# The output stage of a hybrid decoder layer in another written order

## The chip, the core and the metric

The kernel runs on one core of a Trainium2 chip. A core has five engines with queues of their own, which meet only through semaphores: TensorE (PE, matrix products into PSUM), VectorE (DVE), ScalarE (ACT), GpSimd (POOL) and SyncE (SP, which issues most DMAs). Each engine takes its instructions strictly in the order in which the program holds them. The metric is the device time of one execution in microseconds, the median of several runs.

## What is computed

One layer of a decoder, on 1024 positions of width 1024. Cut to what matters here:

```python
m = sigmoid(g_att) * y_att + sigmoid(g_conv) * y_conv
x = x + rms_norm(m @ w_out, norm_mix_post)
h = rms_norm(x, norm_ffn_pre)
a, g = split(causal_dwconv(h @ w_up, conv_ffn_w), 2)
x = x + rms_norm((gelu(g) * a) @ w_down, norm_ffn_post)
```

The change concerns the second and third line, and how the first columns of the fourth are begun.

## The kernel before

All products run in float16, with each operand split in a high and a low half (`hi = f16(s*x)`, `lo = f16(s*x - hi)`) and three products high·high, high·low, low·high (`PASSES`) per pair of tiles. Weights are scaled by a power of two that comes from the sum of their squares. Splitting takes a ScalarE copy (L100) and a VectorE subtraction (L101).

The up-projection uses a two by two block scheme with seven products in place of eight. A `Pair` (class at the end of the file) holds one column tile of `a` and one of `g`; `mm(i)` issues product i (12 matmuls of 128x512, L1682), `take(i)` evicts it. The block operands are the first and second half of the positions (tokens 0 to 3 and 4 to 7, where a token means 128 positions) and of the columns, and sums and differences of these. They lie transposed in `hA` (plain blocks) and `hB` (three sums).

The output stage (end of `mixer`, from L1085) makes these operands. For each token it does

- the product with `w_out`: two halves of 512 columns, each 24 matmuls into one PSUM bank `py` (L1104);
- `taken`: for each half, ScalarE sums the squares (L1111) and VectorE multiplies by the gain into `hn` (L1113);
- `root`: a small VectorE add (L1121, second time L1118) and a power on GpSimd (L1122, L1119);
- `resid`: `x = hn * root + xr`, with `xr` loaded into a weight tile (pool `ws`) and the sum in a tile of pool `xp`, then its store for the last stage (L1126, L1127);
- `squared` (L1130), the second `root`, and `normed`, which gives the normalised row again in `hn` (L1134).

What follows depends on the token. Tokens 0 to 2 are "light": split and transposed by DMA into `hA`. Tokens 4 to 6 are "heavy" (`heavy`): four differences with the light partner, five splits into high (`high`) and low half (`low`), five DMA transposes. Tokens 3 and 7 are transposed on PE (`turned`, L1197) and their halves, sums and differences written from PSUM by ScalarE and VectorE, because they come last. At the same time the weights of the first two pairs, u0 and u1, are split; u1 is loaded, its squares are summed (L57), added up over the partitions by a matmul with ones (`pr`, L83), and split.

What sets the order: the whole stage stands in a `manual_schedule` for PE, ACT, DVE and SP, so the written order is the order on every engine. The tokens come as `seq = (0, 4, 1, 5, 2, 6, 3, 7)`. Operations are called in groups; the steps of `heavy` wait in a list `todo` and are taken from it by `drain(n)` at fixed places of the loop over the tokens. The pool `xp` has four tiles, two of which hold gains throughout the stage; `ws` has four, PSUM eight banks, of which a token takes two.

Of the kernel before, what the change touches and what calls it, by code (L numbers as in the profile page):

```python
# [16 lines left out]
F16 = mybir.dt.float16  # L17
# [17 lines left out]
ENGINES = {mybir.EngineType.PE, mybir.EngineType.Activation, mybir.EngineType.DVE, mybir.EngineType.SP}  # L35
PASSES = ((0, 0), (0, 1), (1, 0))


class Layer:
# [290 lines left out]
    def mixer(self, mid):  # L330
# [753 lines left out]
        seq = (0, 4, 1, 5, 2, 6, 3, 7)  # L1084
        xr, h, sq, ps, y = {}, {}, {}, {}, {}  # L1085
        todo = []

        def drain(n):
            for f in todo[:n]:
                f()  # L1090
            del todo[:n]
# [15 lines left out]
        def taken(tt, nh):  # L1107
# [3 lines left out]
            nc.scalar.activation(self.junk(f"jk_n_post{tt}_{nh}")[:, sl], ps[tt][nh], AF.Square, scale=sgn[:, 25:26],  # L1111
                                 accum_out=sq[tt][:, nh:nh + 1])
            nc.vector.scalar_tensor_tensor(h[tt][:, sl], ps[tt][nh], sgn[:, 24:25], gp_[:, sl], ALU.mult, ALU.mult)  # L1113
# [10 lines left out]
        def resid(tt):  # L1124
            y[tt] = self.xp.tile([P, D], F32, tag="x", name=f"x2_{tt}")
            nc.vector.scalar_tensor_tensor(y[tt], h[tt], sq[tt][:, 3:4], xr[tt], ALU.mult, ALU.add)  # L1126
            nc.sync.dma_start(self.x2[tt], y[tt])  # L1127
# [17 lines left out]
        def light_low(tt):  # L1145
            sub_(hs[tt][:, :, 1], h[tt].rearrange("p (a c) -> p a c", a=2), hs[tt][:, :, 0])
            nc.sync.dma_start_transpose(hA.rearrange("p a l k t -> p (a l k) t")[:, :, ds(tt * P, P)],
                                        hs[tt].rearrange("p a l c -> p (a l c)"))

        def heavy(tt):  # L1150

            A, B = h[tt], h[tt - 4]
# [12 lines left out]
            def high(n, src):  # L1165
                nc.scalar.activation(half(n)[:, :NH], src, AF.Copy)

            def low(n, src):
                sub_(half(n)[:, NH:], src, half(n)[:, :NH])
                nc.sync.dma_start_transpose(dst[n], half(n))  # L1170

            def first():
                sub_(B[:, lo_], A[:, lo_], B[:, lo_])
                high(0, B[:, lo_])

            def second():
                st["c"] = self.wh.tile([P, D], F32, tag="wh", name=f"hs{tt}c")
                sub_(st["c"][:, lo_], A[:, hi_], B[:, lo_])
                high(1, st["c"][:, lo_])
                high(4, A[:, hi_])  # L1180

            def third():
                sub_(A[:, lo_], A[:, hi_], A[:, lo_])
                high(2, A[:, lo_])

            def fourth():
                sub_(B[:, hi_], B[:, hi_], st["c"][:, lo_])
                high(3, B[:, hi_])
            todo.extend([first, second, lambda: low(0, B[:, lo_]), third, lambda: low(1, st["c"][:, lo_]), fourth,
                         lambda: low(4, A[:, hi_]), lambda: low(2, A[:, lo_]), lambda: low(3, B[:, hi_])])  # L1190

# [9 lines left out]

        with tc.manual_schedule(engines=ENGINES):
            load_xr(0)
            load_xr(4)
# [22 lines left out]
            load_xr(1)  # L1227
            begin(1)
            products(1, 0, range(8))
            for tt in (0, 4):  # L1230
                taken(tt, 0), taken(tt, 1)
                root(tt, False)
            resid(0), squared(0)
            resid(4), squared(4)
            root(0, True)
            taken(1, 0)
            normed(0)
            root(4, True)
            light_high(0)
            normed(4)  # L1240
            light_low(0)
            products(1, 1, range(8))
            heavy(4)
            drain(1)
            for m in range(3, 8):
                t, prev = seq[m], seq[m - 1]
                begin(t)
                if m == 6:
                    r = self.scale_sum(sm_u1, 2)
                products(t, 0, range(8))  # L1250
# [24 lines left out]
                root(prev, True)
                if m == 6:
                    self.pair_first("u1")
                drain(1)
                taken(t, 0)
                if m == 5:  # L1280
                    self.sumsq(raw[1], sm_u1[:, 1:2], "u1_1")
                normed(prev)
                if prev == 3:
                    drain(2)
                elif prev < 4:
                    light_high(prev)
                    drain(2)
                    light_low(prev)
                    drain(1)
                else:  # L1290
                    if m == 6:
                        self.pair_sums("u1", self.ws.tile([P, D], F32, tag="ws", name="s12_u1"))
                    heavy(prev)
                    drain(3)
            products(7, 1, range(5))
            turned(3)
            products(7, 1, range(5, 8))
            s3, s7 = ds(3 * P, P), ds(NH + 3 * P, P)

            def b_high(e):  # L1300
                nc.scalar.activation(hA[:, e, 0, :, s3], k_t(pt[3][e]), AF.Copy)

            def b_low(e):
                sub_(hA[:, e, 1, :, s3], k_t(pt[3][e]), hA[:, e, 0, :, s3])
            b_high(0)
            taken(7, 1)
            b_low(0)
            p0.mm(1)
            root(7, False)
            b_high(1)  # L1310
            hq = self.slot([P, 2, KH, P], F32, "hq")
            nc.scalar.activation(hq[:, 0], k_t(pt[3][0]), AF.Copy)
            b_low(1)
            drain(2)
            resid(7)
            p0.take(1)
            squared(7)
            self.pair_part("u1", 2)
            root(7, True)
            p1.mm(1)  # L1320
            p1.take(1)
            normed(7)
            p0.mm(2)
            p0.take(2)
            turned(7)
            p1.mm(2)
            q0, q1 = pt[7]
            tb = [self.slot([P, 2, KH, P], F32, f"tb{e}") for e in range(2)]
# [486 lines left out]
```

## Time and profile before

| | us |
|---|---|
| three runs | 1300.84, 1303.78, 1303.88 (median 1303.78) |
| the profiled execution | 1305.98 |
| its span | 1304.2 |
| mean granted TensorE clock in it | 0.994 |

The span goes from the first to the last instruction of the program in the profile; the time of the execution has 1.8 us around it. In the profile's lists, `x384` is a count, names left of `<-` are written and those right of it read, buffer numbers are left out, and L1104 is a line of the kernel. A bracket at the end of a timeline row holds the idle time of the engine ahead of that row and what ended it. In the table by stretches each engine has its busy time and, behind the x, its instructions; the last three columns are the granted TensorE clock as a share of full speed, the DMA engines' busy share and GB/s.

The page's section 4 follows the work back from the last instruction:

```profile
PE 86%; DVE 8%; ACT 3%; issue 2%; DMA 1%; POOL 0%; SPq 0%; POOLq 0%; DVEq 0%; ACTq 0%
```

The chain runs over TensorE for most of the span; the rest are the places where it waits for the others.

### The profile page before, as it was taken

What the parts mean: (1) busy time and instruction counts of PE and PEld (TensorE: products, weight loads), DVE (VectorE), ACT (ScalarE), POOL (GpSimd) and SP (SyncE); (2) the same over time, 40 slices, a digit from 0 to 9 for tenths busy, and PEclk for the clock granted to TensorE, in tenths of its full rate; (3) what the DMA queues carried; (4) which work ended last, traced back from release to release, by engine and by line L of the source; (5) the groups of instructions that cost most, each with busy time, mean ns of one, the idle gap of its engine ahead of it and who ended that gap; (6) DMA issues with size and microseconds to landing.
All of it is one profiled execution on the core that took longest, in us unless ns stands there. A gap on an engine that the chain in (4) does not pass through costs nothing.

```text
span 1304.2 us, 16771 instructions
## 1 busy us (share of the span) xinstructions
PE 1279.6 (98%) x6450; PEld 581.4 (45%) x6450; DVE 993.5 (76%) x1571; ACT 800.1 (61%) x1136; POOL 48.1 (4%) x67
## 2 busy tenths in 40 slices
PE   9999999999999999999879999999999999999997
PEld 4444444444444444444334444444444444444443
DVE  7488788888878788787768959917963891799767
ACT  6466666665777756654445767746763764677422
POOL 2000000000000000001100000010011001000001
PEclk9999999999999999999989999999999999999999
DMA  6345454453432122516732252274247228622125
GB/s 260 81 81 113 85 119 101 112 111 79 106 100 65 49 81 70 184 32 152 184 106 89 74 232 66 76 135 145 65 116 174 66 72 212 201 65 97 65 98 177
DMA packets 139888, 146.66 MB, mean 112 GB/s; under 512 B 109592, under 2 KB 109728, under 8 KB 139808
## 3 DMA queue, kind: packets, MB, share of 16 engines
q1 hardware_dynamic: 135904, 131.43, 34.6%
q0 software_dynamic: 3888, 14.16, 5.9%
q8 instruction: 50, 0.82, 0.2%
q14 instruction: 30, 0.25, 0.1%
q10 hardware_dynamic: 16, 0.00, 0.0%
HBM read 93.93 MB, written 25.17 MB: 91 GB/s over the span
## 4 chain that ended last, share of the span: by engine, by line
PE 86%; DVE 8%; ACT 3%; issue 2%; DMA 1%; POOL 0%; SPq 0%; POOLq 0%; DVEq 0%; ACTq 0%
PE pd L1488 14%; PE pq L262 3%; PE pcc L262 3%; PE pk L262 3%; PE pywa L662 3%; PE py L1104 3%; PE pywc L662 3%; PE pd L1529 3%; PE pcx L262 2%; PE pcb L262 2%; PE pv L397 2%; PE z L690 2%; PE o L753 2%; DVE R L708 1%; PE pw L420 1%
## 5 line engine op out<-in xcount | busy, mean ns | idle before, releaser
L1682 PEld LDWEIGHTS <-wh_u 128*128 128x128 f16 x1848 | 179.2, 98 | 217.8 <-issue 4.6
L1488 PE MATMUL pd<-wdh,f 128*128 128x512 f16 x864 | 188.8, 379 | 1.2 <-ACT wdh L100 1.2
L1488 PEld LDWEIGHTS <-f 128*128 128x128 f16 x864 | 84.4, 98 | 103.7 <-issue 2.3
L1682 PEld LDWEIGHTS <-wh_g 128*128 128x128 f16 x588 | 56.9, 98 | 68.6 <-issue 0.4
L1104 PE MATMUL py<-wh_wo,m 128*128 128x512 f16 x384 | 86.2, 387 | 0.4 <-DVE wh_wo L101 0.4
L101 DVE SCALAR_TENSOR_TENSOR wh_u<-ws_u,sc,wh_u 128x1024 f16<-128x1024 f32 (+1 forms) x66 | 72.3, 1099 | 11.4 <-ACT wh_u L100 11.4
L100 ACT ACTIVATE wh_u<-ws_u,sc 128x1024 f16<-128x1024 f32 (+1 forms) x66 | 64.5, 998 | 26.4 <-DVE sc L92 12.9
L1502 ACT ACTIVATE y<-pd,sd 128x512 f32<-128x512 f32 x64 | 42.1, 697 | 60.5 <-PE pd L1488 54.0
L694 ACT ACTIVATE R<-z,cz 128x1024 f32<-128x1024 f32 (+3 forms) x48 | 43.1, 898 | 46.5 <-PE z L690 46.5
L1762 DVE SCALAR_TENSOR_TENSOR ugu<-cgu,cw_g,ugu 128x1023 f32<-128x1023 f32 (+1 forms) x44 | 56.3, 1278 | 11.3 <-ACT ugu L1760 11.1
L708 DVE TENSOR_TENSOR_SCAN R<-R,edge 128x256 f32<-128x256 f32 (+3 forms) x64 | 49.2, 810 | 19.3 <-ACT R L694 19.1
L1104 PEld LDWEIGHTS <-m 128*128 128x128 f16 x384 | 38.2, 100 | 51.2 <-issue 8.0
L90 DVE TENSOR_SCALAR sc<-pr 128x1 int32<-128x1 int32 x45 | 6.4, 151 | 71.0 <-PE pr L83 71.0
L1762 DVE SCALAR_TENSOR_TENSOR ua<-cau,cw_a,ua 128x1023 f32<-128x1023 f32 (+1 forms) x44 | 56.2, 1277 | 2.0 <-ACT ua L1760 1.9
L57 ACT ACTIVATE jk_u<-ws_u 128x1024 bf16<-128x1024 f32 x44 | 46.5, 1058 | 4.9 <-DMA ws_u<-w_up_nt 4.3
L695 ACT ACTIVATE be<-z,cz 128x1024 f32<-128x1024 f32 (+3 forms) x48 | 43.0, 896 | 9.4 <-DVE R L727 9.3
L708 DVE TENSOR_TENSOR_SCAN R<-R,cy,zero 128x512 f32<-128x512 f32 x32 | 39.3, 1270 | 10.7 <-ACT R L694 10.7
L717 DVE TENSOR_TENSOR be<-be,R 128x1024 f32<-128x1024 f32 (+3 forms) x48 | 45.7, 951 | 0.1
L727 DVE TENSOR_TENSOR R<-be,R 128x1024 f16<-128x1024 f32 (+3 forms) x48 | 45.7, 951 | 0.0
L262 PE MATMUL pcx<-hT,wh_cx 128*128 128x512 f16 x192 | 44.2, 380 | 0.0
L262 PE MATMUL pcb<-hT,wh_cb 128*128 128x512 f16 x192 | 44.2, 380 | 0.0
L262 PE MATMUL pq<-hT,wh_q 128*128 128x512 f16 x192 | 44.1, 380 | 0.0
(718 smaller groups left out, 2552.3 us busy)
## 6 DMA issues: line engine op xcount, KB each, us to landing
ws_u<-w_up_nt SPq DMA_DIRECT2D x44, 512.0 KB, 3.5
yd<-y POOLq DMA_DIRECT2D x24, 512.0 KB, 5.5
ds<-w_down SPq DMA_DIRECT2D x22, 512.0 KB, 5.6
wd<-w_down SPq DMA_DIRECT2D x22, 512.0 KB, 3.6
ws_g<-w_in_nt SPq DMA_DIRECT2D x14, 512.0 KB, 3.5
x<-x SPq DMA_DIRECT2D x8, 512.0 KB, 10.0
ws_wo<-w_out SPq DMA_DIRECT2D x8, 512.0 KB, 6.1
xr<-x SPq DMA_DIRECT2D x8, 512.0 KB, 3.9
```

What stands on the lines that cost most here:

```text
L57: self.nc.scalar.activation(self.junk(f"jk_{name}")[:, :w], src, AF.Square, accum_out=acc)
L100: self.nc.scalar.activation(dst[:, 0, :], src, AF.Copy, scale=s)
L101: self.nc.vector.scalar_tensor_tensor(dst[:, 1, :], src, s, dst[:, 0, :], ALU.mult, ALU.subtract)
L262: nc.tensor.matmul(ps, w[:, wi, ds(k * P, P)], hT[:, hi, k, ds(c * NH, NH)], start=n == 0, stop=n == last)
L662: nc.tensor.matmul(ps, w[0][:, wi, ds((d % 2) * NH + k * P, P)], acts[bi][k][:, hi, ds(c * NH, NH)], start=n == 0, stop=n == 11)
L708: nc.vector.tensor_tensor_scan(rev, rev, first, 0.0 if u["top"] else carry[tl][:, h, :], ALU.mult, ALU.add)
L717: nc.vector.tensor_tensor(t["be"][:, :, :W], t["be"][:, :, :W], t["R"][:, :, 1:W + 1], ALU.mult)
L727: nc.vector.tensor_tensor(wv[1], be[:, :, :W], wv[0], ALU.subtract)
L1104: nc.tensor.matmul(ps[tt][nh], m16[k][:, hi, ds(tt * P, P)], wo[k][:, wi, ds(nh * NH, NH)], start=k == 0 and p == 0, stop=k == 7 and p == 2)
L1488: nc.tensor.matmul(banks[n][:, :cw], f16[g][k][:, hi, ds(tt * P, P)], w[k][:, wi, ds(c0, cw)], start=(hi, wi) == (0, 0) and k == 0, stop=( ...
L1682: nc.tensor.matmul(ps, w[wt][:, wi, ds(wc * NH + k * P, P)], l.block(i, hi, k), start=first and n == 0, stop=n == 3 * KH - 1, skip_group_c ...
L1762: nc.vector.scalar_tensor_tensor(u[:, lag:], c[:, :T - lag], sm[:, 2 - lag:3 - lag], u[:, lag:], ALU.mult, ALU.add)
```

## The change

The groups of the stage are taken apart into single operations, each with a short name in a table `op`: `P31` is the second half of token 3's product, `q` the sum of squares of a half, `g` its gain, `r`/`R` the two roots, `x` the residual, `Y` its store, `s` the second square, `n` the normed row, `X` the load; `H`, `L`, `D` a light token's high half, low half and transpose; `a` to `d`, `h`, `l`, `D` with a number a heavy token's; `T` the transposes on PE; `u`, `v` the weight parts of the first two pairs; `p` and `E` products and evictions of these pairs. A list of 225 names gives the order, and a loop runs through it. The tokens come as 0, 1, 4, 5, 3, 2, 6, 7. The residual's input is loaded into the tile that takes the sum; for the first two tokens that is a `ws` tile, for the others one of `xp`. Before the list stand only the last parts of `w_out` and the products of tokens 0 and 1, interleaved by k.

```diff
+TOKENS = (0, 1, 4, 5, 3, 2, 6, 7)
+OUT_ORDER = (
...
+    "d5 D51 h53 l53 D54 n3 P60 q21 r2 g21 D53 x2 Y2 s2 X6 P61 j0 R2 j1 n2 q60 ut H2 g60 v1 L2 T3 X7 q61 "
+    "v2 D2 um P70 th0 r6 g61 th1 tl0 up tq x6 vh0 tl1 Y6 s6 vl0 P71 q70 R6 v3 v4 g70 n6 a6 b6 h60 c6 h61 "
+    "p01 l60 q71 l61 D60 vh2 r7 g71 h62 vl2 p11 E01 h64 x7 vh3 l62 Y7 s7 p02 l64 D62 d6 E11 R7 vl3 D61 "
+    "h63 l63 E02 D64 n7 T7 p12 t1 D63 t2 k1 tr e1 k2 t3 p05 vh1 e2 t4 k3 k5 e3 k4 vl1 p15 E12 E05 e5 e4 "
+    "E15 "
+)
...
-        seq = (0, 4, 1, 5, 2, 6, 3, 7)
...
         def load_xr(tt):
-            xr[tt] = self.ws.tile([P, D], F32, tag="ws", name=f"xr{tt}")
-            nc.sync.dma_start(xr[tt], a["x"][ds(tt * P, P), :])
+            n = TOKENS.index(tt)
+            pool, tag = (self.ws, "ws") if n < 2 else (self.xp, "x")
+            y[tt] = pool.tile([P, D], F32, tag=tag, name=f"x2_{tt}")
+            nc.sync.dma_start(y[tt], a["x"][ds(tt * P, P), :])
...
         def resid(tt):
-            y[tt] = self.xp.tile([P, D], F32, tag="x", name=f"x2_{tt}")
-            nc.vector.scalar_tensor_tensor(y[tt], h[tt], sq[tt][:, 3:4], xr[tt], ALU.mult, ALU.add)
+            nc.vector.scalar_tensor_tensor(y[tt], h[tt], sq[tt][:, 3:4], y[tt], ALU.mult, ALU.add)
+
+        def stored(tt):
             nc.sync.dma_start(self.x2[tt], y[tt])
...
+        def part_high(n, i, pool, tag):
+            w = pool.tile([P, 2, D], F16, tag=tag, name=f"wh_{n}_{i}")
+            self.pw[n][0][i] = w[:, :, :NH] if i == 3 else w
+            nc.scalar.activation(self.pw[n][0][i][:, 0], source(n, i), AF.Copy, scale=self.pscale[n])
+
+        def part_low(n, i):
+            w = self.pw[n][0][i]
+            nc.vector.scalar_tensor_tensor(w[:, 1], source(n, i), self.pscale[n], w[:, 0], ALU.mult, ALU.subtract)
...
-            self.pair_first("u0")
-            for i in (2, 1, 3):
-                self.pair_part("u0", i)
-            begin(0), begin(4)
+            for tt in TOKENS:
+                begin(tt)
             for k in range(8):
-                for tt in (0, 4):
+                for tt in TOKENS[:2]:
                     for nh in range(2):
                         products(tt, nh, [k])
...
-            for m in range(3, 8):
-                t, prev = seq[m], seq[m - 1]
...
-            products(7, 1, range(5))
-            turned(3)
-            products(7, 1, range(5, 8))
...
+            for name in OUT_ORDER.split():
+                op[name]()
             self.pair_fetch("u2")
```

Every engine holds the same instructions as before, and up to the stage and behind it in the same order. Three places show what moves. The names below are the program's: `py_0`, `py_1` the two halves of a token's product, `pt` the transposes on PE, `pr` the sum for u1's scale, `m_k` the k-th tile of the left operand.

TensorE before, at the sum for the scale, which stands between the two halves of token 3 (`py_0_5832`, `py_1_5833`), and then at token 3's transposes, which stand inside the second half of token 7 (`py_1_5928`):

```order
L1104 MATMUL py_0_5832<-wh_wo_5347,m_7_5338 128x512
L83 LDWEIGHTS ones
L83 MATMUL pr_5862<-rb_5835,ones 128x1
L1104 LDWEIGHTS m_0_4508
L1104 MATMUL py_1_5833<-wh_wo_5258,m_0_4508 128x512
```

```order
L1104 MATMUL py_1_5928<-wh_wo_5334,m_4_4875 128x512
L1197 MATMUL pt_0_6000<-ident,hn_5908 128x128 x4
L1197 MATMUL pt_1_6001<-ident,hn_5908 128x128 x4
L1104 LDWEIGHTS m_5_5060
L1104 MATMUL py_1_5928<-wh_wo_5340,m_5_5060 128x512
```

TensorE now, behind the second half of token 6 (`py_1_5370`) and ahead of token 7 (`py_0_5372`), where token 3 is `hn_5760`:

```order
L1111 MATMUL py_1_5370<-wh_wo_5347,m_7_5338 128x512
L1210 MATMUL pt_0_5903<-ident,hn_5760 128x128 x4
L1210 MATMUL pt_1_5904<-ident,hn_5760 128x128 x4
L95 LDWEIGHTS ones
L95 MATMUL pr_5919<-rb_5893,ones 128x1
L1111 LDWEIGHTS m_0_4508
L1111 MATMUL py_0_5372<-wh_wo_5258,m_0_4508 128x512
```

Both have one place now, 14 halves into the stage: the sum comes one half later than before, the transposes one half and 15 matmuls earlier, while token 3's own products come four halves earlier.

VectorE before, from the gain of token 7's second half (`hn_5976`) to its normed row and the first reader of its transposes (`tb`):

```order
L1113 SCALAR_TENSOR_TENSOR hn_5976<-py_1_5928,sgn,g_post 128x512
L1137 TENSOR_TENSOR hA<-pt_0_6000,hA 128x4x128
L1121 TENSOR_SCALAR r_post_5926<-r_post_5926 128x1
L1137 TENSOR_TENSOR hA<-pt_1_6001,hA 128x4x128
L1126 SCALAR_TENSOR_TENSOR x_7_6043<-hn_5976,r_post_5926,xr_5966 128x1024
L101 SCALAR_TENSOR_TENSOR wh_u_2_6051<-s_u_5913,sc_5834,wh_u_2_6051 128x1024
L1118 TENSOR_SCALAR r_post_5926<-r_post_5926 128x1
L1134 SCALAR_TENSOR_TENSOR hn_5976<-x_7_6043,r_post_5926,g_ffn 128x1024
L1137 TENSOR_TENSOR tb_6108<-pt_0_6086,hq 128x512
```

VectorE now, at the same place (token 7 is `hn_5994`; `hs6b`, `hs6c` and `hn_5806` are halves of token 6's operands):

```order
L1131 TENSOR_SCALAR r_post_5371<-r_post_5371 128x1
L1123 SCALAR_TENSOR_TENSOR hn_5994<-py_1_5373,sgn,g_post 128x512
L1275 SCALAR_TENSOR_TENSOR wh_u_2_6022<-s_u_5900,sc_5892,wh_u_2_6022 128x1024
L1135 SCALAR_TENSOR_TENSOR x_7_5913<-hn_5994,r_post_5371,x_7_5913 128x1024
L1148 TENSOR_TENSOR hs6b<-hn_5898,hs6b 128x512
L1148 TENSOR_TENSOR hs6c<-hn_5898,hs6c 128x512
L1148 TENSOR_TENSOR hn_5806<-hn_5806,hs6c 128x512
L1128 TENSOR_SCALAR r_post_5371<-r_post_5371 128x1
L1275 SCALAR_TENSOR_TENSOR wh_u_3_6048<-ws_u_0_5812,sc_5892,wh_u_3_6048 128x512
L1148 TENSOR_TENSOR hs6b<-hn_5806,hs6b 128x512
L1145 SCALAR_TENSOR_TENSOR hn_5994<-x_7_5913,r_post_5371,g_ffn 128x1024
L1148 TENSOR_TENSOR tb_6103<-pt_0_6081,hq 128x512
```

Token 3's copies have left this place; a whole weight part stands ahead of the residual, and three operations of token 6, half a weight part and one more operation of token 6 stand between the residual and the normed row.

SP now, around the store of token 7 (`x2d_5300`), with the five transposes of token 6 about it; before, that store stood behind all five:

```order
L1138 DMA x2d_5299<-x_6_5857 128x1024
L1191 DMA_TRANSPOSE hB_5290<-hs6a 128x8x128
L1138 DMA x2d_5300<-x_7_5913 128x1024
L1191 DMA_TRANSPOSE hB_5290<-hs6b 128x8x128
L1191 DMA_TRANSPOSE hB_5290<-hs6a 128x8x128
L1191 DMA_TRANSPOSE hA<-hs6c 128x8x128
L1191 DMA_TRANSPOSE hA<-hs6b 128x8x128
```

The store moved ahead of four transposes; those now wait on SP until the residual of token 7 is there.

More of the change, by code (lines that the diff above doesn't have):

```diff
@@ L1105, in products, with squared_half, gained @@
                                      start=k == 0 and p == 0, stop=k == 7 and p == 2)
[L1107 removed]
+        def squared_half(tt, nh):
+            sl = ds(nh * NH, NH)
+            nc.scalar.activation(self.junk(f"jk_n_post{tt}_{nh}")[:, sl], ps[tt][nh], AF.Square, scale=sgn[:, 25:26],
+                                 accum_out=sq[tt][:, nh:nh + 1])
+        def gained(tt, nh):
             if nh == 0:
@@ L1163, in half, with source, high, low @@
                 return st[t][:, n % 2]
[L1165 to L1169, printed above, removed]
+            def source(n):
+                if n == 1:
+                    return st["c"][:, lo_]
+                return {0: h[tt - 4][:, lo_], 2: h[tt][:, lo_], 3: h[tt - 4][:, hi_], 4: h[tt][:, hi_]}[n]
+            def high(n):
+                nc.scalar.activation(half(n)[:, :NH], source(n), AF.Copy)
+            def low(n):
+                sub_(half(n)[:, NH:], source(n), half(n)[:, :NH])
+            def turn(n):
                 nc.sync.dma_start_transpose(dst[n], half(n))
-            def first():
-                sub_(B[:, lo_], A[:, lo_], B[:, lo_])
-                high(0, B[:, lo_])
             def second():
                 st["c"] = self.wh.tile([P, D], F32, tag="wh", name=f"hs{tt}c")
[L1178 to L1190, printed above, removed]
+                sub_(st["c"][:, lo_], h[tt][:, hi_], h[tt - 4][:, lo_])
+            op[f"a{tt}"] = lambda: sub_(h[tt - 4][:, lo_], h[tt][:, lo_], h[tt - 4][:, lo_])
+            op[f"b{tt}"] = second
+            op[f"c{tt}"] = lambda: sub_(h[tt][:, lo_], h[tt][:, hi_], h[tt][:, lo_])
+            op[f"d{tt}"] = lambda: sub_(h[tt - 4][:, hi_], h[tt - 4][:, hi_], st["c"][:, lo_])
+            for n in range(5):
+                op[f"h{tt}{n}"] = lambda n=n: high(n)
+                op[f"l{tt}{n}"] = lambda n=n: low(n)
+                op[f"D{tt}{n}"] = lambda n=n: turn(n)
         pt = {}
@@ new lines, in last_part @@
+        def last_part(n):
+            sm, ua, ug, s12 = self.praw[n]
+            sub_(ua[:, ds(NH, NH)], ua[:, ds(NH, NH)], s12[:, ds(NH, NH)])
+        whs, o16s = (self.wh, "wh"), (self.o16p, "o16")
+        for c, n in (("u", "u0"), ("v", "u1")):
+            for i in range(4):
+                home = o16s if c == "v" and i > 1 else whs
+                op[f"{c}h{i}"] = lambda n=n, i=i, home=home: part_high(n, i, *home)
+                op[f"{c}l{i}"] = lambda n=n, i=i: part_low(n, i)
+        op["us"] = lambda: last_part("u0")
@@ new lines, in mixer, with v_load, v_total, v_across @@
+        op["v4"] = lambda: last_part("u1")
+        v = {}
+        def v_load():
+            v["raw"] = []
+            for i, src in enumerate(self.psrc["u1"]):
+                v["raw"].append(self.ws.tile([P, D], F32, tag="ws", name=f"ws_u1_{i}"))
+                nc.sync.dma_start(v["raw"][i], src)
+            v["sm"] = self.small("sm_u1")
+            self.praw["u1"] = v["sm"], *v["raw"]
+        def v_total():
+            v["r"] = self.scale_sum(v["sm"], 2)
+        def v_across():
+            v["r"] = self.scale_mm(*v["r"])
@@ new lines, in v_power, with v_first, v_second @@
+        def v_power():
+            self.pscale["u1"], inv = self.scale_pow(*v["r"], 1)
+            self.pw["u1"] = [None] * 4, inv
+        def v_first():
+            v["s12"] = self.ws.tile([P, D], F32, tag="ws", name="s12_u1")
+            ua, ug = v["raw"]
+            nc.vector.tensor_tensor(v["s12"][:, lo_], ug[:, lo_], ug[:, hi_], ALU.add)
+        def v_second():
+            sub_(v["s12"][:, hi_], v["s12"][:, lo_], v["raw"][0][:, lo_])
+            self.praw["u1"] = v["sm"], *v["raw"], v["s12"]
@@ L1311, in mixer @@
[L1311 to L1328, printed above, removed]
```

179 lines of the change are left out of this document (60 added, 119 removed), and 4 rows, old and new, of the table OUT_ORDER.

## The prediction

> **What bounds the kernel now.** I read the busy line of the page first, then the list of who waited for whom on TensorE.
>
> ```profile
> PE 1279.6 (98%) x6450; PEld 581.4 (45%) x6450; DVE 993.5 (76%) x1571; ACT 800.1 (61%) x1136; POOL 48.1 (4%) x67
> ```
>
> ```profile
> PE pt L1197 <- DVE hn L1134: 6.5, 2, 5.6
> PE pr L83 <- DVE rb L74: 3.5, 1, 3.5
> PE pu0a L1682 <- DVE hA L1137: 2.1, 1, 2.1
> PE pd L1488 <- ACT wdh L100: 1.2, 2, 0.7
> ```
>
> TensorE is busy for 98% of the span, so only its waits can be won (columns: total, times, longest). The three largest groups lie in the output stage, the part that the diff rewrites. The timeline of TensorE shows them in place, the wait in brackets:
>
> ```profile
> 564.92 67.28 PE L1104 MATMUL py<-wh_wo,m 128*128 128x512 f16 x311 [0.37 <-DVE wh_wo L101]
> 635.69 0.16 PE L83 MATMUL pr<-rb,ones 128*128 128x1 bf16 x1 [3.49 <-DVE rb L74]
> 635.72 15.44 PE L1104 MATMUL py<-wh_wo,m 128*128 128x512 f16 x63
> 656.72 1.97 PE L1197 MATMUL pt<-ident,hn 128*128 128x128 f32 x8 [5.56 <-DVE hn L1134]
> 658.48 3.06 PE L1104 MATMUL py<-wh_wo,m 128*128 128x512 f16 x9
> 661.38 0.38 PE L1682 MATMUL pu0a<-hA,wh_u 128*128 128x512 f16 x1
> 663.86 4.19 PE L1682 MATMUL pu0a<-hA,wh_u 128*128 128x512 f16 x11 [2.09 <-DVE hA L1137]
> 667.88 2.75 PE L1682 MATMUL pu1a<-hA,wh_u 128*128 128x512 f16 x12
> ...
> 674.14 1.09 PE L1197 MATMUL pt<-ident,hn 128*128 128x128 f32 x8 [0.91 <-DVE hn L1134]
> 675.07 2.75 PE L1682 MATMUL pu1a<-hA,wh_u 128*128 128x512 f16 x12
> 677.66 2.75 PE L1682 MATMUL pu0c<-hB,wh_u 128*128 128x512 f16 x12
> ```
>
> Four waits: 3.49 + 5.56 + 2.09 + 0.91 = **12.05 us**. The matmuls behind the first three are also slow. Twelve at full rate take 677.66 − 675.07 = 2.59 us, 0.216 each. So 63 of them with 0.16 us of tail should take 13.77 and took 15.44 (1.67 lost); the eight transposes at 656.72 needed 1.76 to the next row where those at 674.14 needed 0.93 (0.83); nine took 2.90 for 1.94 (0.96); eleven took 4.02 for 2.38 (1.64). Together **5.10 us**. The granted clock (the column before the last two) says why, and the same table shows the vector engine:
>
> ```profile
> 590.00:615.00 25.00, 25.00 (x118) 11.33 (x117) 18.97 (x27) 11.26 (x21) 5.20 (x6) 1.00 0.60 154
> 615.00:640.00 25.00, 21.51 (x94) 9.33 (x93) 16.60 (x29) 12.91 (x25) 3.08 (x5) 0.93 0.98 228
> 640.00:665.00 25.00, 17.34 (x73) 8.20 (x72) 17.23 (x26) 9.29 (x19) 2.76 (x4) 0.84 0.50 134
> 665.00:690.00 25.00, 24.09 (x111) 11.02 (x110) 14.78 (x24) 14.81 (x26) 0.55 (x1) 0.96 0.29 106
> 690.00:715.00 25.00, 25.00 (x119) 11.35 (x118) 24.38 (x36) 13.80 (x16) 0.00 (x0) 1.00 0.14 43
> 715.00:740.00 25.00, 25.00 (x120) 11.39 (x119) 24.37 (x46) 20.40 (x30) 0.00 (x0) 1.00 0.19 63
> ```
>
> The clock is below 1 in the three stretches with the long waits and full elsewhere. At most 12.05 + 5.10 = **17.15 us** can be won here. VectorE has room in the stage: 18.97 + 16.60 + 17.23 + 14.78 = 67.6 us busy in 100.
>
> **The change part by part.** No engine gets another instruction; every matmul, copy, subtraction and DMA is there as before, in another order. So each edit costs or gains only by when PE finds its operand. I place the new order on the old times: without its first short wait the stage's row of matmuls begins at 564.92 − 0.22 = 564.7, and a half token (24 matmuls) takes 5.18 us.
>
> The **sum for the scale** (pr) stood after 13 halves and now stands after 14 and the first transposes, at 564.7 + 14 × 5.18 + 0.93 = 638.2.
>
> ```profile
> 635.48 0.16 DVE L74 CAST rb<-sc 128x1 bf16<-128x1 f32 x1
> 648.16 0.67 ACT L1111 ACTIVATE jk_n_post<-py,sgn 128x512 bf16<-128x512 f32 x1
> 652.67 0.69 DVE L1137 TENSOR_TENSOR hn<-hn,hs6c 128x512 f32<-128x512 f32 x1
> 655.39 1.28 DVE L1134 SCALAR_TENSOR_TENSOR hn<-x,r_post,g_ffn 128x1024 f32<-128x1024 f32 x1
> ```
>
> Even at its old time, 635.48 + 0.16, the operand is 2.5 us early: 3.49 us go. The loads behind it keep their place on SP, with 20 DMAs of the stage ahead of them where 18 were.
>
> **Token 3**, the first to be transposed on PE, moves from seventh to fifth. Its last square began at 648.16 and its normed row ended at 656.67, 8.5 us. Its products now end after 10 halves (616.5) and its transposes come after 14 (637.2), so 20.7 us lie between: 5.56 us go. The copies of the transposed halves then have from 637.2 to the first up-projection product after 16 halves, 564.7 + 16 × 5.18 + 0.96 = 648.5. That is 11.3 us; before, the product was released 7.14 us after the transposes began (656.72 to 663.86), a stay behind token 7's square included: 2.09 us go.
>
> Token 2 takes token 3's old place in the row and reaches the up-projection by a DMA transpose:
>
> ```profile
> 622.31 0.67 ACT L1111 ACTIVATE jk_n_post<-py,sgn 128x512 bf16<-128x512 f32 x1
> ...
> 636.38 1.65 SPq L1147 DMA_TRANSPOSE hA<-hs  x1
> ```
>
> Its second square began at 622.31, its transpose 14.1 us later; with the 6.0 us of the slowest landing (below) that is 20.1. Its products now end after 12 halves, 626.9, which leaves 21.6 us. Covered by 1.5 us against the slowest landing; if that goes, the first product waits.
>
> The weight parts of the first pair, now split among the first squares, are read from 648.5 on, some 60 us after they are made. The residual added in place is the same VectorE instruction, and GpSimd keeps its 16 powers in the same pairs. Both cost nothing.
>
> **Token 7** decides what is left. Old rows of its chain:
>
> ```profile
> 661.64 0.69 ACT L1111 ACTIVATE jk_n_post<-py,sgn 128x512 bf16<-128x512 f32 x1 [3.18 <-PE py L1104]
> 662.46 0.75 DVE L1113 SCALAR_TENSOR_TENSOR hn<-py,sgn,g_post 128x512 f32<-128x512 f32 x1 [4.59 <-ACT jk_n_post L1111]
> ...
> 664.68 1.28 DVE L1126 SCALAR_TENSOR_TENSOR x<-hn,r_post,xr 128x1024 f32<-128x1024 f32 x1 [0.15 <-POOL r_post L1122]
> ...
> 668.58 1.05 ACT L1130 ACTIVATE jk_n_ffn<-x 128x1024 bf16<-128x1024 f32 x1
> ...
> 669.62 1.14 ACT L100 ACTIVATE wh_u<-s_u,sc 128x1024 f16<-128x1024 f32 x1
> ...
> 670.79 1.28 DVE L101 SCALAR_TENSOR_TENSOR wh_u<-s_u,sc,wh_u 128x1024 f16<-128x1024 f32 x1 [4.83 <-ACT wh_u L100]
> ...
> 671.99 0.15 DVE L1118 TENSOR_SCALAR r_post<-r_post 128x1 f32<-128x1 f32 x1
> 672.22 0.55 POOL L1119 TENSOR_TENSOR r_post<-r_post,neghalf 128x1 f32<-128x1 f32 x1 [7.57 <-DVE r_post L1118]
> 672.80 1.28 DVE L1134 SCALAR_TENSOR_TENSOR hn<-x,r_post,g_ffn 128x1024 f32<-128x1024 f32 x1 [0.67 <-POOL r_post L1119]
> ```
>
> Call E the first up-projection matmul (661.38 there). VectorE is released by the square at E + 1.08 and does a small add and the gain (0.75) by E + 2.0; its instructions start some 0.08 before the end of the one ahead (670.79 + 1.28 against 671.99). In the new order a low half of a weight (1.28) stands ahead of the residual and waits for ScalarE's high half, which starts behind the square and takes 1.14: low half from E + 2.1, residual from E + 3.3 to E + 4.6. The residual's square takes ScalarE 1.05, to E + 5.8; VectorE meanwhile runs three half-width operations (0.69 each, 0.61 apart), so the second small add stands at E + 6.3. GpSimd's power brings its result 0.81 later, E + 7.1. Ahead of the normed row stand a half-width weight part (0.75, as the gain) and a low part of token 6 (0.69), for which ScalarE's copy comes at E + 7.1 (it starts behind the three operations and takes as long as the square); the normed row runs from E + 7.8 to E + 9.0, and PE may transpose at E + 9.1. It now has three products of 2.59 us before that, so it stands there at E + 7.8: **1.3 us** of waiting stay, where 0.91 was. Without the fillers the chain would be 6.7 us long and the wait nothing; that is the lower end.
>
> Does that wait drop the clock? The trace lets 0.91 us pass and slows the matmuls behind 2.09 us, by 1.64 us; 1.3 us lies between and nearer the first, so I take no drop and keep 1.64 us for the range. [...]
>
> **DMA.** Loads of the residual now land in the tile that takes the sum. From the third token on that tile is one of two, so a load waits for the store and the normed row of the token two places before.
>
> ```profile
> x2d<-x SPq DMA_DIRECT2D x8, 512.0 KB, 3.3
> xr<-x SPq DMA_DIRECT2D x6, 512.0 KB, 3.9
> hA<-hs5c SPq DMA_TRANSPOSE x1, 6.0
> ```
>
> Store and load take 7.2 us at these medians; the next use comes two tokens later, 20.7 us. Covered. Token 7's store now stands on SP ahead of four transposes of token 6; with 1.65 us of SP each (the row above), behind the store at E + 4.9, the last is issued at about E + 10 and lands within 6.0 us, E + 16; the first product that reads one of them comes at E + 17.8 (9.1 + 0.93 + 3 × 2.59). Covered, with 1.8 us to spare.
>
> **Sum.** 17.15 − 1.3 = 15.8 us. The profiled execution took 1305.98 us (1.8 around its span), so it would take 1290.2; the median of the three runs, 1303.78, lies 2.2 lower, so I predict **1288.0 us**.
>
> **The rivals.**
>
> 1. The remaining wait drops the clock. For: 2.09 us did. Against: 0.91 did not. Price 1.64: 1289.6.
> 2. One of the old waits stays, because a step named above slips behind another on ScalarE or VectorE. The largest is token 3's, 5.56 + 0.83 + 0.96 = 7.35: 1295.4; the smallest, 3.49 + 1.67: 1293.2. Against: the margins of 2 to 12 us.
> 3. The time comes back in the feed-forward. VectorE is 97% busy from 690 to 740 (48.75 of 50), and PE already waits 0.7 there. If its work slips by half the gain, 1296; by all, 1303.8, no change. Against: it has 32 us of idle in the 100 before and needs to give up 16, and the later steps stand in the same order.
> 4. Slower: the two residual tiles throttle the stage. If a load with the store ahead of it took over 20.7 us instead of 7.2, each of the two generations behind would stall PE; from 20.7 + 9.9 on, twice, the 15.8 are gone and 3.9 more with them, 1307.7 or worse. For: the DMA share of 0.98 between 615 and 640. Against: it would take four times the medians.
>
> **How the numbers follow.** A measurement here can tell about 0.3% (3.9 us) from no change. Forecast 0.64, rival 1 0.20, rival 2 0.07, rival 3 0.06 (half of it no change), rival 4 0.03. Faster is 0.64 + 0.20 + 0.07 + 0.03 = 0.94, same 0.03, slower 0.03. The low end is the whole 17.15 with the 2.9 us by which the fastest run lies below the median, 1284; the high end takes in rival 1 with the 2.2 us by which the profiled execution lies above the median (1291.8) and the cheaper end of rival 2, 1294.
>
> **What would show it.** Right: no wait for rb, none for hA, one wait for hn of 1 to 2 us, clock 1.00 all through the stage, every later row some 16 us earlier. Wrong: a transpose group with over 2 us ahead of it, a new wait on a DMA in the chain, or waits of pd above 3 us.

## The result, and the profile after

The changed kernel takes 1289.55 us (median of 4 runs, 1286.51 to 1289.74) against 1303.83 us of the kernel before (4 runs, 1300.84 to 1303.97): a ratio of 0.989, interval 0.987 to 0.9911. The forecast was 1288.0. The two profiled executions took 1305.98 and 1289.63 us, 16.35 less, where the working had 15.8.

The waits of TensorE in the profile after (columns: total, times, longest):

```profile
PE pd L1475 <- ACT wdh L112: 1.1, 2, 0.7
PE pt L1210 <- DVE hn L1145: 1.1, 1, 1.1
```

The waits for `rb` and `hA` are gone, and of the two for a normed row one of 1.10 us is left. Its place in the timeline of TensorE after the change:

```profile
565.11 72.46 PE L1111 MATMUL py<-wh_wo,m 128*128 128x512 f16 x335 [0.42 <-DVE wh_wo L113]
637.41 1.04 PE L1210 MATMUL pt<-ident,hn 128*128 128x128 f32 x8
638.28 0.17 PE L95 MATMUL pr<-rb,ones 128*128 128x1 bf16 x1
638.31 10.52 PE L1111 MATMUL py<-wh_wo,m 128*128 128x512 f16 x48
648.66 2.75 PE L1669 MATMUL pu0a<-hA,wh_u 128*128 128x512 f16 x12
...
657.70 1.09 PE L1210 MATMUL pt<-ident,hn 128*128 128x128 f32 x8 [1.10 <-DVE hn L1145]
```

335 matmuls run in one piece, then token 3's transposes, the sum for the scale and 48 more without a stop. From the start of the long row to token 7's transposes it is 657.70 − 565.11 = **92.59 us**; before it was 674.14 − 564.92 = **109.22**. This stretch serves below as the measure of the output stage, since an execution's own beginning varies by up to 3.4 us (last section). The table by stretches, after (columns as in the prediction's: TensorE, weight loads, VectorE, ScalarE, GpSimd, granted clock, DMA share, GB/s):

```profile
615.00:640.00 25.00, 25.00 (x122) 11.82 (x121) 19.59 (x33) 13.35 (x27) 3.12 (x5) 1.00 1.02 242
640.00:665.00 25.00, 23.90 (x115) 11.21 (x114) 23.57 (x36) 16.98 (x29) 3.06 (x3) 1.00 0.60 150
```

The clock is 1.00 in both, where it was 0.93 and 0.84. Between 640 and 665 VectorE works 23.57 of 25 us, where it had 17.23: its row has hardly a gap left.

**Where the time went.** Waits: 12.05 before, 1.10 after, 10.95 less. Slow matmuls: 5.10 before, none after. That is 16.05 of the 16.63. The rest is the last matmul ahead of each stop: one alone takes 0.38 us (the row at 661.38 before) where one in a row takes 0.216, so each of four stops cost 0.16 more than its bracket shows, and only one is left: 3 × 0.16 = 0.5. That leaves 0.1 open.

Two more views say why the waits were there. The chain that ends last, taken between 604 and 657 us and summed by line, of before and of after (the list ends where the view cuts it off):

```profile
by line: issue 16.2%; DVE hn L1134 11.6%; DVE x L1126 9.8%; DMA ws_u<-w_up_nt 9.1%; DVE hn L1113 7.2%; ACT jk_n_post L1111 6.1%; ACT jk_n_ffn L1130 5.4%; POOL r_post L1122 4.5%; DVE hs L1137 4.3%; DVE hn L1137 3.6%; DVE wh_u L101 2.4%; SPq 
```

```profile
by line: PE py L1111 83.1%; issue 3.2%; DVE x L1135 2.4%; DVE hs6b L1148 2.4%; DVE hn L1145 2.3%; ACT wh_u L1271 2.0%; PE pt L1210 1.6%; DVE wh_u L1275 1.3%; DVE hs6c L1148 1.1%; DVE hn L1148 1.1%; ACT jk_n_post L1116 0.6%; DVE r_post L1128
```

Before, no product of TensorE is in the chain: it runs from VectorE to ScalarE to GpSimd and back, with a load in it, and 16.2% of it is "issue", time in which the next engine waited for nothing that the profile shows. After, 83.1% is TensorE. And the squares of the products on ScalarE, before (L1111) and after (L1116), over the whole stage, with what ScalarE waited for ahead of them (total, times):

```profile
L1111 ACT ACTIVATE jk_n_post<-py,sgn x16: 666/670/688, 585.7 to 661.6; 128x512 bf16<-128x512 f32 x16
...
  PE py L1104: 3.2, 1
```

```profile
L1116 ACT ACTIVATE jk_n_post<-py,sgn x16: 671/687/688, 583.9 to 648.9; 128x512 bf16<-128x512 f32 x16
...
  PE py L1111: 15.8, 9
```

Before, ScalarE waited for a product once in 16 squares, ahead of the last: the other products lay ready and ScalarE came late. After, it waits for TensorE 9 times in 16.

### The profile page after: what moved, and what is told of

It is laid out like the page before. It is cut to its first block, busy times and chain, and to the rows that moved or that the text cites. A ratio compares the mean times of both kernels' runs of the same rounds, so it can differ in the third digit from the quotient of the medians.

```text
span 1287.7 us, 16771 instructions
## 1 busy us (share of the span) xinstructions
PE 1274.1 (99%) x6450; PEld 579.7 (45%) x6450; DVE 992.3 (77%) x1571; ACT 800.4 (62%) x1136; POOL 46.3 (4%) x67
## 4 chain that ended last, share of the span: by engine, by line
PE 90%; DVE 6%; ACT 2%; issue 1%; DMA 1%; POOLq 0%; DVEq 0%; POOL 0%; ACTq 0%
PE pd L1475 14%; PE py L1111 6%; PE pq L274 3%; PE pcc L274 3%; PE pk L274 3%; PE pywa L674 3%; PE pywc L674 3%; PE pd L1516 3%; PE pcx L274 3%; PE pcb L274 2%; PE pv L409 2%; PE z L702 2%; PE o L765 2%; DVE R L720 1%; PE pw L432 1%
## 5 line engine op out<-in xcount | busy, mean ns | idle before, releaser
L1111 PE MATMUL py<-wh_wo,m 128*128 128x512 f16 x384 | 83.4, 379 | 0.4 <-DVE wh_wo L113 0.4
L113 DVE SCALAR_TENSOR_TENSOR wh_u<-ws_u,sc,wh_u 128x1024 f16<-128x1024 f32 (+1 forms) x60 | 65.7, 1099 | 8.8 <-ACT wh_u L112 8.7
L112 ACT ACTIVATE wh_u<-ws_u,sc 128x1024 f16<-128x1024 f32 (+1 forms) x60 | 58.6, 998 | 21.6 <-DVE sc L104 12.9
L1111 PEld LDWEIGHTS <-m 128*128 128x128 f16 x384 | 37.5, 98 | 45.7 <-issue 0.7
```

Of the source, the lines that this page charges most:

```text
L112: self.nc.scalar.activation(dst[:, 0, :], src, AF.Copy, scale=s)
L113: self.nc.vector.scalar_tensor_tensor(dst[:, 1, :], src, s, dst[:, 0, :], ALU.mult, ALU.subtract)
L1111: nc.tensor.matmul(ps[tt][nh], m16[k][:, hi, ds(tt * P, P)], wo[k][:, wi, ds(nh * NH, NH)], start=k == 0 and p == 0, stop=k == 7 and p == 2)
```

## The experiments

**1. One wait alone.** In the kernel before, the sum for the scale one half token later:

```diff
-                if m == 6:
-                    r = self.scale_mm(*r)
                 if m < 7:
                     products(t, 1, range(8))
+                if m == 6:
+                    r = self.scale_mm(*r)
+                if m < 7:
                     load_xr(t)
```

> The kernel before, with one product moved: the sum for the scale (pr) goes behind the second half of token 3's products instead of between its halves, 24 matmuls (5.18 us) later. Theory A (the waits of TensorE have separate causes, as the prediction's sum adds them): the wait for rb (3.49 us) and the slow clock behind it (1.67) go, the other waits stay (5.56, 2.09, 0.91); profiled time 1300.8 instead of 1305.98. Theory B (the waits are pieces of one lag: VectorE and ScalarE run a chain from token to token, and TensorE is ahead of it wherever it stands): the wait for rb goes and the wait for token 3's normed row grows by the same 3.49 + 1.67, to 10.7 us; time as before within 0.5 us.

1304.80 us (12 runs) against 1304.79, ratio 0.9997 (0.9985 to 1.0008). TensorE's timeline:

```profile
562.36 72.46 PE L1104 MATMUL py<-wh_wo,m 128*128 128x512 f16 x335 [0.94 <-DVE wh_wo L101]
634.66 0.17 PE L83 MATMUL pr<-rb,ones 128*128 128x1 bf16 x1
634.69 8.58 PE L1104 MATMUL py<-wh_wo,m 128*128 128x512 f16 x39
654.21 1.97 PE L1197 MATMUL pt<-ident,hn 128*128 128x128 f32 x8 [10.94 <-DVE hn L1134]
...
672.18 1.09 PE L1197 MATMUL pt<-ident,hn 128*128 128x128 f32 x8 [0.45 <-DVE hn L1134]
```

The wait for `rb` is gone and the next one is 10.94 us instead of 5.56. The stretch is 109.82, no shorter. What one wait loses, the next one gains, as theory B had it: the waits of before look like one lag, seen at several places. Theory A falls.

**2. The old token order, with the new single operations.** The list is the changed kernel's, but each place is taken by the token that had this position before; the light and heavy groups follow their tokens, and token 3's transposes come behind the last product:

```diff
-TOKENS = (0, 1, 4, 5, 3, 2, 6, 7)
+TOKENS = (0, 4, 1, 5, 2, 6, 3, 7)
...
+    "H2 L2 D2 P30 q61 r6 g61 D53 x6 Y6 s6 X3 P31 j0 R6 j1 n6 q30 ut g30 v1 X7 q31 v2 um P70 a6 b6 r3 g31 h60 "
+    "c6 h61 up x3 vh0 Y3 s3 vl0 P71 q70 R3 v3 v4 g70 n3 T3 th0 th1 tl0 tq tl1 p01 l60 q71 l61 D60 vh2 r7 g71 "
```

> The changed kernel's single operations with the old token order (0,4,1,5,2,6,3,7): each operation takes the place that the token in the same position had, the light and heavy groups follow their tokens, and token 3's transposes come after the last product instead of after 14 halves. Theory 'order of tokens': the gain comes from token 3 being early; then its waits come back nearly whole (5.56 + 2.09 and the clock), time 1297 to 1300. Theory 'placing': the gain comes from the single operations; time within 1 us of the changed kernel's 1289.6. Mine: both; 16 halves end at about 647.6, token 3's last products at 637.2, so its chain of 8.5 us is just covered, but the copies of its transposed halves (first one needed 1.5 to 2 us after the transposes) are not, and token 7 comes later behind them: 3 to 5 us of waits in all, profiled time 1292.5 to 1295.

1288.85 us, ratio 0.9875 (0.9861 to 0.9889). TensorE's waits for normed rows and `hA` in the timeline:

```profile
562.15 72.46 PE L1110 MATMUL py<-wh_wo,m 128*128 128x512 f16 x335 [0.63 <-DVE wh_wo L112]
...
645.36 1.09 PE L1209 MATMUL pt<-ident,hn 128*128 128x128 f32 x8 [0.36 <-DVE hn L1144]
646.70 0.38 PE L1668 MATMUL pu0a<-hA,wh_u 128*128 128x512 f16 x1 [0.25 <-ACT hA L1236]
647.42 2.53 PE L1668 MATMUL pu0a<-hA,wh_u 128*128 128x512 f16 x11 [0.35 <-DVE hA L1147]
...
656.79 1.09 PE L1209 MATMUL pt<-ident,hn 128*128 128x128 f32 x8 [1.65 <-DVE hn L1144]
```

The stretch is 94.64 us: 2.05 more than with the new order, 14.6 less than before. My 3 to 5 us were too many; the single operations, with the residual in place (worth nothing by itself, experiment 7), carry seven eighths of the gain, the token order and the later transposes 2 us. The median doesn't show these 2 us, since in the profiled execution the long row begins 2.96 us earlier than in that of the changed kernel.

**3. Tokens 2 and 3 exchanged** in the changed kernel, token 2's light group behind its normed row:

```diff
-TOKENS = (0, 1, 4, 5, 3, 2, 6, 7)
+TOKENS = (0, 1, 4, 5, 2, 3, 6, 7)
```

> The changed kernel with tokens 2 and 3 exchanged (0,1,4,5,2,3,6,7), their operations exchanged in place, and token 2's light group behind its normed row. Token 3's last products then end at 626.9 and its transposes stay at 637.2, 10.3 us later, against a chain of 8.5 us: no wait of TensorE returns, time 1289.6 within 0.5 us. Theory 'order of tokens': every place that token 3 is later costs; with 5.18 us less cover some of its old wait of 5.56 returns, time 1291.5 or more, and a wait for hn ahead of token 3's transposes.

1286.52 us (1286.32 to 1289.87), 3 us below the median of the changed kernel above; but the long row of this profile also begins 3.0 us earlier. The stretch is 654.73 − 562.13 = 92.60 us, as with the new order:

```profile
562.13 72.46 PE L1111 MATMUL py<-wh_wo,m 128*128 128x512 f16 x335 [0.60 <-DVE wh_wo L113]
...
654.73 1.09 PE L1210 MATMUL pt<-ident,hn 128*128 128x128 f32 x8 [1.10 <-DVE hn L1145]
```

**4. The wait that is left.** Three VectorE operations go behind token 7's normed row: the low halves of two weight parts (`vl2`, `vl3`) and a low half of token 6 (`l63`). The transpose `D63`, which the expectation counts as a fourth, stood behind it already:

```diff
-    "p01 l60 q71 l61 D60 vh2 r7 g71 h62 vl2 p11 E01 h64 x7 vh3 l62 Y7 s7 p02 l64 D62 d6 E11 R7 vl3 D61 "
-    "h63 l63 E02 D64 n7 T7 p12 t1 D63 t2 k1 tr e1 k2 t3 p05 vh1 e2 t4 k3 k5 e3 k4 vl1 p15 E12 E05 e5 e4 "
+    "p01 l60 q71 l61 D60 vh2 r7 g71 h62 p11 E01 h64 x7 vh3 l62 Y7 s7 p02 l64 D62 d6 E11 R7 D61 "
+    "h63 E02 D64 n7 T7 p12 l63 t1 D63 t2 k1 tr e1 vl2 k2 t3 p05 vh1 e2 t4 k3 k5 e3 k4 vl1 p15 vl3 E12 E05 e5 e4 "
```

> The changed kernel with four operations moved behind token 7's normed row and transposes: the low halves of two weight parts of the second pair (vl2, vl3), and a low half of token 6 with its transpose (l63, D63). If these stand for the 1.10 us that TensorE still waits for token 7's normed row: the wait is gone, no other takes its place, profiled time 1288.5 (span 1286.6). Rival: the chain of token 7 is only handed on, TensorE waits as long for the halves of hB behind the transposes or for the weight part that now comes later, time 1289.6 or more.

1286.97 us (1285.44 to 1288.47). The wait is gone and none follows:

```profile
565.08 72.46 PE L1111 MATMUL py<-wh_wo,m 128*128 128x512 f16 x335 [0.45 <-DVE wh_wo L113]
...
656.41 1.06 PE L1210 MATMUL pt<-ident,hn 128*128 128x128 f32 x8
657.31 2.75 PE L1669 MATMUL pu1a<-hA,wh_u 128*128 128x512 f16 x12
```

The stretch is 91.33 us, 1.26 less. This and the changed kernel once more, side by side:

> The changed kernel once more, beside e10 on one chip. Expected: wait of 1.10 us ahead of token 7's transposes again, 92.6 us from the first of the row to them; times between 1286.3 and 1289.9, spread by when TensorE's clock becomes full in the first 12 us of the execution, not by the output stage.

> The version of e4 once more, beside e9 on one chip. If its gain is real: no wait ahead of token 7's transposes, the stretch 91.3 us, and the median 1 to 1.5 us below that of e9. If e4 was lower by chance of the start: the same median as e9 within 0.5 us, or the wait back.

Medians 1287.09 (1286.24 to 1288.56) and 1287.26 (1285.02 to 1288.35): no difference in four runs each. The profiles again show the wait of 1.10 in the one and none in the other; from the 48 matmuls behind the sum for the scale to the first matmuls into `pu1b` (second pair) it is 38.26 us in the changed kernel both times and 36.97 in this version both times. So the stage is 1.29 us shorter, and a median of four runs, spread over 2 to 3 us, can't tell it.

**5. Foreign work out of the lag.** In the kernel before, the second pair's first weight part and its sums go behind token 3's normed row:

```diff
-                if m == 6:
-                    self.pair_first("u1")
...
-                    if m == 6:
-                        self.pair_sums("u1", self.ws.tile([P, D], F32, tag="ws", name="s12_u1"))
...
+            self.pair_first("u1")
+            self.pair_sums("u1", self.ws.tile([P, D], F32, tag="ws", name="s12_u1"))
             products(7, 1, range(5))
```

> The kernel before, with the first weight part of the second pair (a high half on ScalarE, a low half on VectorE) and the three half-width operations of its sums moved out of the step of token 3, to just ahead of token 7's second products in the written order. TensorE's work is not touched. Measured from the first of the long row of product matmuls to token 7's transposes, before 564.92 to 674.14, 109.2 us. Theory B (one lag of VectorE and ScalarE): the chain of waits of before has 1.05 + 1.28 + 0.61 + 0.54 + 0.68 = 4.2 us of these operations between token 6's residual and token 3's, so the wait ahead of token 3's transposes shrinks from 5.56 to about 2 and the stretch to 105 to 106 us. Theory A (token 3 stands too late in TensorE's row for its own chain of 8.5 us): these operations belong to another tensor, the wait stays 5 to 6 us and the stretch 109 us.

1299.18 us, ratio 0.997 (0.9955 to 0.9985). TensorE's timeline:

```profile
562.14 67.28 PE L1104 MATMUL py<-wh_wo,m 128*128 128x512 f16 x311 [0.78 <-DVE wh_wo L101]
632.85 0.16 PE L83 MATMUL pr<-rb,ones 128*128 128x1 bf16 x1 [3.42 <-DVE rb L74]
...
650.65 1.09 PE L1197 MATMUL pt<-ident,hn 128*128 128x128 f32 x8 [2.42 <-DVE hn L1134]
...
666.55 1.09 PE L1197 MATMUL pt<-ident,hn 128*128 128x128 f32 x8 [0.91 <-DVE hn L1134]
```

The wait ahead of token 3's transposes falls from 5.56 to 2.42, the stretch to 104.41 us (105 to 106 were expected; the transposes and the nine matmuls behind them, at a granted clock of 1.00, also take 0.93 and 1.94 us to the next row where they took 1.76 and 2.90, 1.8 us less). Token 3's place in TensorE's row is untouched.

**6. Three links.** The same, and:

```diff
-                if m == 5:
-                    self.sumsq(raw[0], sm_u1[:, 0:1], "u1_0")
...
+                normed(prev)
                 taken(t, 0)
                 if m == 5:
-                    self.sumsq(raw[1], sm_u1[:, 1:2], "u1_1")
-                normed(prev)
+                    for i in range(2):
+                        self.sumsq(raw[i], sm_u1[:, i:i + 1], f"u1_{i}")
```

> The kernel before with the edit of e5 and two more: the normed row of a token stands ahead of the next token's first square and gain instead of behind them, and the two sums of squares of the second pair's weights stand together behind that square, so that ScalarE no longer waits there for their load. TensorE's order, the tokens' order and the number of instructions stay as before. Theory B: each link takes its own microseconds out of one lag; from 109.2 to about 102 us for the stretch from the first of the row to token 7's transposes, the wait for rb 1 to 2 us, the wait ahead of token 3's transposes about 3 us. Theory A: waits for rb and for token 3's row stay within 1 us of 3.49 and 5.56, the stretch stays 108 to 110.

1297.47 us, ratio 0.9949 (0.9933 to 0.9965). Waits of TensorE:

```profile
PE pt L1197 <- DVE hn L1134: 4.0, 2, 3.1
PE pu0a L1679 <- DVE hA L1137: 1.9, 1, 1.9
PE pr L83 <- DVE rb L74: 1.8, 1, 1.8
```

From the long row at 565.40 to token 7's transposes at 668.11 it is 102.71 us, 6.5 less than before, with TensorE's order and the token order as they were. Theory B holds: VectorE and ScalarE had run behind, and shortening their links takes time out: 4.8 us of the stretch by the first (experiment 5), 1.7 more by the other two together. A part of what the wait for `rb` lost (3.42 to 1.77) came back at token 3 (2.42 to 3.14), as in experiment 1. Of the 6.5 us, 4.3 are waits (12.05 to 7.75); the rest are slow matmuls.

**7. A tile of its own for the residual**, in the changed kernel:

```diff
-            y[tt] = pool.tile([P, D], F32, tag=tag, name=f"x2_{tt}")
-            nc.sync.dma_start(y[tt], a["x"][ds(tt * P, P), :])
+            xr[tt] = self.ws.tile([P, D], F32, tag="ws", name=f"xr{tt}")
+            nc.sync.dma_start(xr[tt], a["x"][ds(tt * P, P), :])
...
+            y[tt] = self.xp.tile([P, D], F32, tag="x", name=f"x2_{tt}")
```

> The changed kernel with the residual's input loaded into a tile of its own (ws), and the sum written to an xp tile, as before the change. If the residual in place is worth nothing by itself: stretch from the first of the row to token 7's transposes 92.6 us as in the changed kernel, no new wait of TensorE. Rival: eight residual tiles and the second pair's three tiles turn over one pool, the second pair's load comes later and the sum for its scale too; a wait for rb returns, stretch 94 us or more.

1288.40 us (1287.91 to 1289.25). Here the long row begins without a stop, one matmul earlier, at 563.36, and token 7's transposes at 656.20: 92.84, less that matmul 92.62. One wait of 1.10, no other in the stage. The residual in place gains nothing by itself.

**8. A longer wait, for the clock.** In the changed kernel, half of the third up-projection product behind token 7's transposes (a `p02` cut by k):

```diff
+    "p01 l60 q71 l61 D60 vh2 r7 g71 h62 vl2 p11 E01 h64 x7 vh3 l62 Y7 s7 p020 p021 l64 D62 d6 E11 R7 vl3 D61 "
+    "h63 l63 D64 n7 T7 p022 p023 E02 p12 t1 D63 t2 k1 tr e1 k2 t3 p05 vh1 e2 t4 k3 k5 e3 k4 vl1 p15 E12 E05 e5 e4 "
...
+        for k in range(KH):
+            op[f"p02{k}"] = lambda k=k: p0.mm(2, range(k, k + 1))
```

> The changed kernel with half of the third up-projection product (6 matmuls, 1.30 us) moved behind token 7's transposes, and its eviction behind it. The wait ahead of them grows from 1.10 to 2.4 us. [...]

1289.34 us (1286.95 to 1292.42). In the profiled execution the wait is 2.39 us and nothing behind it is slow; from the 48 matmuls to the first into `pu1b` it is 39.56 us, 1.30 more than in the changed kernel, just the time of the six matmuls:

```profile
656.49 1.09 PE L1210 MATMUL pt<-ident,hn 128*128 128x128 f32 x8 [2.39 <-DVE hn L1145]
...
658.72 2.75 PE L1671 MATMUL pu1a<-hA,wh_u 128*128 128x512 f16 x12
```

The granted clock is 1.00 from 640 to 680 us of this execution. The four times (1286.95, 1289.23, 1289.45 and 1292.42) lie up to 5.5 us apart; only the execution of 1289.45 has a trace, so whether the slowest had a drop of the clock is not shown. The last section sets this wait beside those of the other runs.

## Why the prediction was right

- **The sum.** 17.15 us were to be had and 1.3 to stay; 1.10 stayed, no matmul was slow, and the profiled execution came to 1289.63 where 1290.2 was worked out. Not in the sum: 0.16 us at the end of the last matmul ahead of each stop, 0.5 in all.
- **The clock.** "I take no drop" held: 1.00 throughout. Rival 1 did not come. The reason given, that 1.3 us is nearer to 0.91 than to 2.09, was an estimate from two waits, and the runs bear it out only in part: waits of 1.65, 1.77 and 1.93 us passed as well, but so did 2.39 and 2.42, while one of 2.00 was followed by a clock of 0.50 (last section). The length of a wait alone does not decide it; what does was not shown.
- **Token 7.** With E = 648.66, the chain goes as worked out: gain, low half, residual, square, normed row, and the transposes at 657.70 = E + 9.04 (E + 9.1 was forecast). The wait is 1.10 and not 1.3, since TensorE's last matmul ends 0.16 later than the start-to-start count says. GpSimd's power took 0.98 us where 0.55 was taken over, and did not matter, since VectorE was still busy. Experiment 4 shows that three of the operations ahead of the normed row are enough to cause the wait.
- **Sum for the scale, token 3, first product.** 638.28, 637.41 and 648.66 against 638.2, 637.2 and 648.5.
- **The residual in place, DMA.** Worth nothing, costs nothing (experiment 7); no wait of TensorE on a DMA in the stage, so rival 4 did not come.
- **Rival 3.** The waits of `pd` are 1.1 us in all, as before (1.2): the feed-forward gave nothing back. The first matmuls into `pu1b` come at 676.57 where they came at 693.01, 16.4 us earlier ("some 16").

Two steps of the working gave the right sum for a reason that the runs do not bear out. It took the waits one by one, 3.49 for a place in the row, 5.56 for token 3's move from seventh to fifth. Experiment 1 took the first away and the second grew by 5.4 us, about the 3.49 and the 1.67 of slow matmuls behind it. So the prices of rival 2, "one of the old waits stays", are not those of single waits: as far as the lag of VectorE and ScalarE is not worked off, it is paid at the next wait. And token 3's place was not what its 5.56 us hung on: experiment 5 took 3.1 of them without moving it, experiment 2 left 0.36 with the token in its old place and its transposes only nine matmuls later. The view that would have told this stood in the profile of before: ScalarE waited for a product once in 16 squares, and the chain had no product of TensorE in it from 604 to 657 us. That the new order works the whole lag off, the prediction did not work out: it had VectorE's 32 us of idle time in 100 and the chains of three tokens. That the sum came out so close was in this part luck.

The gain is thus mainly the packing of VectorE's and ScalarE's rows: an engine seldom stands at an operation whose operand is late while another lies ready behind it. How the 14.6 us divide among the single moves was followed for three of them in the old code (6.5 us in all, experiment 6); the rest was not taken apart.

## What to carry to other kernels

When one engine waits at several places, ask first whether it is ahead of a common lag: if the engines that feed it seldom wait for it (here once in 16 squares), removing one wait makes the next longer (5.56 to 10.94 us in experiment 1), and only shortening the feeding engines' rows gains time (6.5 us in experiment 6). Put each operation of an in-order engine where its operand is ready (in the kernel before, 24 matmuls stood 3.49 us behind the sum for the scale; in experiment 1 they ran ahead of it), with work of another tensor between an operation and the one that needs its result, and keep that work from standing ahead of the last chain. Judge a change of a microsecond by a stretch between two named instructions, not by the median of a few executions.

## What the runs showed of the hardware

**The clock in the stage.** In before the granted clock is 0.50 in three stretches of the stage, 3.41, 6.82 and 3.41 us long from 636.52, 653.59 and 663.83 us, and 1.00 around them (columns: TensorE busy, clock, DMA share, GB/s):

```profile
636.52:639.93 3.41, 3.41 (x10) 0.50 1.12 231
639.93:643.35 3.42, 3.42 (x17) 1.00 0.82 287
...
653.59:657.00 3.41, 0.28 (x2) 0.50 1.00 255
657.00:660.41 3.41, 3.41 (x13) 0.50 1.14 248
660.41:663.83 3.42, 1.35 (x6) 1.00 0.17 38
663.83:667.24 3.41, 3.38 (x9) 0.50 0.13 55
667.24:670.65 3.41, 3.41 (x17) 1.00 0.74 252
```

Each begins inside one of TensorE's waits or up to 0.83 us behind its end; in experiments 1, 5 and 6 up to 1.16 us behind it. The waits of over 1 us where the clock was read, and the 0.91 of before, each with its end and the clock of 0.50 that came with it:

| run | TensorE waits for | us | ends at | clock 0.50 |
|---|---|---|---|---|
| before | `rb` | 3.49 | 635.69 | 636.52 to 639.93 |
| before | token 3's normed row | 5.56 | 656.72 | 653.59 to 660.41 |
| before | `hA` | 2.09 | 663.86 | 663.83 to 667.24 |
| before | token 7's normed row | 0.91 | 674.14 | none |
| after | token 7's normed row | 1.10 | 657.70 | none |
| after, run once more | token 7's normed row | 1.10 | 654.06 | none |
| experiment 1 | token 3's normed row | 10.94 | 654.21 | 646.42 to 660.07 |
| experiment 1 | `hA` | 2.00 | 662.33 | 663.49 to 666.90 |
| experiment 2 | token 7's normed row | 1.65 | 656.79 | none |
| experiment 5 | `rb` | 3.42 | 632.85 | 632.72 to 636.13 |
| experiment 5 | token 3's normed row | 2.42 | 650.65 | none |
| experiment 5 | `hA` | 2.34 | 656.24 | 656.61 to 660.02 |
| experiment 6 | `rb` | 1.77 | 634.45 | none |
| experiment 6 | token 3's normed row | 3.14 | 651.37 | 650.56 to 657.39 |
| experiment 6 | `hA` | 1.93 | 659.49 | none |
| experiment 8 | token 7's normed row | 2.39 | 656.49 | none |

So 2.09 us of waiting cost 1.64 us more in before, and 1.93, 2.39 and 2.42 us cost nothing more in experiments 6, 8 and 5, while 2.00 and 2.34 us in experiments 1 and 5 came with a slow stretch. The length of the wait does not order these rows, and no run shows what does.

**The first 12 us spread the times.** In two executions of the same instructions, of before and of experiment 1:

```profile
6.83 4.02 PE L420 MATMUL pw<-ones 128*128 128x512 bf16 x9
10.65 1.65 PE L409 MATMUL pt_pre<-ident,x 128*128 128x128 f32 x8
```

```profile
5.85 2.12 PE L420 MATMUL pw<-ones 128*128 128x512 bf16 x9
7.80 1.04 PE L409 MATMUL pt_pre<-ident,x 128*128 128x128 f32 x8
```

Nine matmuls take 0.42 us each in the one and 0.217 in the other. In experiment 6 nine take 0.427 each at a granted clock of 0.50 (653.13 to 656.97); here the clock column has 1.00 in both, so a lower clock in the first 12 us is an estimate from the times of the matmuls. 2.9 us between the two rows of transposes become 2.6 us at the long row (564.92 and 562.36), and 1.8 us are left in the whole time, the stage of experiment 1 being 0.6 longer. Over all profiles the first product of the output stage begins between 560.99 and 564.36 us. The profiled executions of before and after are both late ones (564.92 and 565.11), so their difference is fair. The four runs before and after the change spread by about as much, 3 us; other groups of runs spread by 0.6 to 6.7 us, so the start may not be all of it. This is how the forecast's median came out 1.55 us too low: it put the median 2.2 us below the profiled execution, as before the change, and after it the two came out alike (1289.55 and 1289.63), while the profiled execution was 0.6 us faster than worked out. The changed kernel run once more has its median at 1287.09.
